# A hybrid decoder layer on one core: the third block's first product moved ahead of the first block's last one, a later fourth operand, an own tile for the last residual, more zero matmuls at the start

## The chip, the cores and the metric

The kernel runs on one core of a Trainium2 chip. The engines named below are PE (TensorE: matmuls; PEld are its weight loads), DVE (VectorE), ACT (ScalarE), POOL (GpSimd) and SP (SyncE, which issues most of the DMAs). The metric is the device time of one execution in microseconds (us), lower is better; the time before is the median of three runs.

## The reference

One layer over 1024 tokens of width 1024, in float32. `rms_norm` divides a row by its root mean square and multiplies it by a gain.

```python
def swiglu(h, w_gate, w_up, w_down):
    return (jax.nn.silu(h @ w_gate) * (h @ w_up)) @ w_down
...
        x = x + 0.5 * swiglu(rms_norm(x, ffn1_norm[i]), ffn1_w_gate[i], ffn1_w_up[i], ffn1_w_down[i])
        h = rms_norm(x, mix_norm[i])
        fq, fk, fv, f_logit, sq, sk, sv, g_fox, g_sb = split_columns(h @ w_in[i])
        ...
        merged = (jax.nn.sigmoid(g_fox) * (y_fox @ w_branch_fox[i])
                  + jax.nn.sigmoid(g_sb) * (y_sb @ w_branch_sb[i]))
        x = x + merged @ w_out[i]
        x = x + 0.5 * swiglu(rms_norm(x, ffn2_norm[i]), ffn2_w_gate[i], ffn2_w_up[i], ffn2_w_down[i])
        x = x + jax.nn.sigmoid(rms_norm(x, ple_norm[i]) @ w_ple_gate[i]) * (p[i] @ w_ple_proj[i])
```

The hidden width of the two feed-forward halves is 2816. `y_fox` and `y_sb` are two causal attentions, which the change does not touch.

## The kernel before

**Four stages of the same form.** Four large products of a normalized activation with a weight are computed by one helper, `make_up`: gate and up of the first feed-forward half (from 0 us), the gate columns of the mixer (from about 680 us), gate and up of the second half (from about 1540 us) and the gate of the last step, called PLE (from about 2160 us). What comes ahead of such a stage and fills its operands is here called its entry. In the first entry the activation comes from `x` in rows and is turned by PE; in the other three it comes from the stage before, already turned.

**Seven products a block.** The weight is cut in blocks n of 256 columns; in the feed-forward halves even n are gate columns and odd n up columns. A block's product with the activation is done as a 2 by 2 scheme with seven half-size products m = 1 to 7 in place of eight. A product is written (n, m) below. Operand B[m] of the activation is shared by all blocks; the weight's operand of (n, m) is made by `prep(n, m)`. Each operand is a float32 array split in two of a shorter format: an upper part, cast by ACT (line 649 for B, line 105 for weights), and the rest, subtracted by DVE (line 653 for B, line 106 for weights). A product is 12 matmuls of 128x512 (line 617): four with both upper parts, four with the activation's rest, four with the weight's rest.

**The order.** Nothing is scheduled by the compiler in these stages: `manual_schedule` keeps each engine in the order of the program. `up_order` lists the products; step s runs product s of that list, then `evict` of that product, then `begin(s)`, then `prep` of the product four steps later. For the blocks 1 and 2 the order is written out, with block 0 done before it without the scheme (`plain`). Step 5 is (1, 7), 6 is (2, 5), 7 is (1, 3), 8 is (2, 7) and 9 is (1, 4).

**What an eviction does.** After (n, 7) ACT copies the bank (lines 782, 1319, 1741), and DVE adds bank "d", the sum of (n, 5), to it (lines 783, 1320, 1742). The product (n, 3) goes into that same bank "d", so (1, 3) waits for this addition. In the gate blocks and in all blocks of the mixer and PLE an ACT function follows (lines 790, 1321, 1743). After (n, 1) ACT copies the bank into a new tile of `E[n]` (line 778).

**The fourth operand.** B[4] serves (n, 4) alone. It is made in four pieces j: `combo_d(j)` takes a difference in place (DVE; lines 731 and 732 in the first entry, line 734, one instruction, in the others) and `combo_e(j)` splits it (ACT 649, DVE 653). In the first entry a piece is a quarter of the tokens, so that each matmul needs all four; in the others a piece is one of the four sums over features, so that the matmuls come upon the pieces one after another. `begin(s)` calls both by the step.

**The front.** `busy(n)` issues n matmuls on a tile of zeros (line 253); the first call only clears the tile. `spread` copies the gain to all partitions by matmuls with one row (line 239), and DVE copies it back (241). Then DVE normalizes the rows (268), PE turns them (273), ACT casts (282) and DVE subtracts (287) to fill B[1] and B[2].

**The end.** In PLE the eight row blocks of the output are finished by `finish(n, i)`: a multiplication (1718), and the addition of x either inside a DMA (line 1720, issued by POOL) or on DVE (1722) with an x fetched into a tile (`fetch(..., True)`, line 1713); `store` (1726) writes it. The table `AT` says at which step each is called. `slot(tag, ...)` gives the next of a ring of buffers with that name; a new user waits for the last reader of the old one.

Of the kernel before, what the change touches and what calls it, by code (L numbers as in the profile page):

```python
# [18 lines left out]
P = 128  # L19
# [17 lines left out]
def tile_hybrid_decoder_layer(  # L37
# [484 lines left out]
                wd_sums(c, (1, 2, None, 3, 4)[i])  # L522
        return types.SimpleNamespace(sums=sums, wd_block=wd_block, wd_sums=wd_sums, load_hid=load_hid, operand=operand, prep=prep, product=product, chunks=chunks)

    def up_order(nm_):

        seqn = [(2, 1), (1, 5), (2, 2), (1, 6), (2, 6), (1, 7), (2, 5), (1, 3), (2, 7), (1, 4)]
        for n in range(3, nm_ - 1):
            seqn += [(n, 1), (n - 1, 4), (n, 2), (n - 1, 3), (n, 6), (n, 5), (n, 7)]
        n = nm_ - 1  # L530
        return seqn + [(n, 1), (n - 1, 4), (n, 2), (n, 6), (n, 5), (n, 7), (n - 1, 3), (n, 3), (n, 4)]

    def make_up(N, src, nm_, tags, first_fn, first_done=None, over=None):
# [50 lines left out]
        def last_sum(n, eng=nc.gpsimd):  # L584
            eng.tensor_sub(part(n, 2), part(n, 2), part(n, 6))
# [46 lines left out]
        def rows():  # L632
            return "rows" in N[0]
# [102 lines left out]
        def combo_e(j):  # L736
            if j == 0:
                B[4] = home(4)
            high(4, j, w(j, 0))
            low(4, j, w(j, 0))  # L740

        def begin(s):

            if s == 0:
                sums(2, nc.vector, True)
            elif s == 1:
                for q in range(4):
                    combo_s(q, 7)
            elif s == 2:
                last_sum(1, nc.vector)  # L750
            elif s == 3:
                third_sum(2, nc.vector)
            elif s == 7:
                last_sum(2, nc.vector)
            for j in range(4):
                if s == (j + 2 if rows() else 2 + j // 2):
                    combo_d(j)
            if 3 < s < 8:
                combo_e(s - 4)
        return types.SimpleNamespace(a=combo_a, b=combo_b, t=combo_t, l=combo_l, u=combo_u, s=combo_s, load=load, prep=prep, sums=sums, last_sum=last_sum, plain=plain, silu=silu, product=product, begin=begin, E=E, B=B, bank_of=bank_of)  # L760

    def ffn(N, wg, wu, wd, resid, hid, tags, entry, tail):
# [2 lines left out]
        wdown = wd[0].rearrange("(j k p) n -> k p j n", k=2, p=P)  # L765
        LA = 4
        nm_ = 2 * NF
        seqn = up_order(nm_)
        U = make_up(N, lambda n: wsrc[n % 2][:, :, n // 2 * 256:n // 2 * 256 + 256], nm_, tags, AF.Silu)
        E = U.E  # L770

        def evict(n, m, ps):
            up, j = n % 2, n // 2
            if m == 1:
                E[n] = [slot(t, [P, 2, 512]) for t in (("GF", "RN"), ("Y", "Y"))[up]]
            e1, e2 = E[n]
            if m == 1:
                nc.scalar.copy(e1[:, 0, :], ps[:])
            elif m == 6:
                nc.scalar.copy(e1[:, 1, :], ps[:])  # L780
            elif m == 7:
                nc.scalar.copy(e2[:, 1, :], ps[:])
                nc.vector.tensor_add(e2[:, 1, :], e2[:, 1, :], U.bank_of[n, "d"][:])  # L783
            elif m == 2:
                nc.vector.tensor_add(e1[:, 0, :], e1[:, 0, :], ps[:])
            elif m == 3:
                nc.vector.tensor_add(e1[:, 1, :], e1[:, 1, :], ps[:])
            if not up:
                if m == 7:
                    nc.scalar.activation(e2[:, 1, :], e2[:, 1, :], AF.Silu)  # L790
                elif m == 4:
                    nc.scalar.activation(e2[:, 0, :], ps[:], AF.Silu)
                elif m == 3:
                    nc.scalar.activation(e1[:], e1[:], AF.Silu)
                return
            g1, g2 = E[n - 1]
            if m == 7:
                nc.vector.tensor_mul(g2[:, 1, :], g2[:, 1, :], e2[:, 1, :])
            elif m == 4:
                nc.vector.tensor_mul(g2[:, 0, :], g2[:, 0, :], ps[:])  # L800
                nc.sync.dma_start(hid[j, :, 1:3, :], g2[:])
            elif m == 3:
                nc.vector.tensor_mul(g1[:], g1[:], e1[:])  # L803
                nc.sync.dma_start(hid[j, :, 0, :], g1[:, 0, :])
# [718 lines left out]
    def first_entry(F):  # L1523
# [11 lines left out]
        N.append(rows_begin(X[1], gB))  # L1535
        N[0]["B"] = [slot("H", [P, 2, 4, 512], F32R) for _ in range(2)]
        busy(0)
        busy(6)
        spread(N[0]["g"])
        for t in range(1, 4):  # L1540
            load_x(t)
# [6 lines left out]
        for t in range(4):  # L1548
            rows_stat(N[0], t, ("PT", "WL", "WL", "PT")[t], True)
            rows_mul(N[0], t)  # L1550
        busy(4)
        rows_high(N[0], 0, ps1)
        rows_high(N[0], 1, ps1)
        rows_low(N[0], 0)
# [56 lines left out]
                fn(j)  # L1611
        F.prep(1, 6)

    tags = {"raw": {1: ("KH", "KL")}, "sum": {}, "w": ("Q", "Q", "KH", "KL"), "hl": ("WL", "WL", "WL", "WH") + ("PT",) * 4 + ("WL", "WL", "WL", "PT"), "B": {"12": "X", 3: ("T",) * 4, 5: "H", 6: "H", 7: "X", 4: "X"}}
    ffn(N, ffn1_w_gate, ffn1_w_up, ffn1_w_down, xs, ad[0], tags, first_entry, mix_start())
    gqk = cp.tile([P, 1], F32, name="gqk")
    nc.sync.dma_start(gqk[0:HD, :], q_norm[0].unsqueeze(1))
# [87 lines left out]
    def ple_start():  # L1705
# [26 lines left out]
        def evict(n, m, ps):  # L1732
# [19 lines left out]
            elif m == 4:  # L1752
# [1 line left out]
        F.evict = evict  # L1754
        late = (slice(0, 512), False)
        AT = {6: [(fetch, 1, 0, "Q"), (fetch, 1, 1, "WH")], 7: [(finish, 0, 0)], 8: [(finish, 0, 1), (fetch, 3, 0, "Q", True), (fetch, 2, 1, "T")],
              9: [(fetch, 3, 0, "T")], 10: [(finish, 1, 0)], 11: [(finish, 1, 1), (fetch, 3, 1, "Q"), (store, 0, 0)], 12: [(store, 0, 1), (fetch, 3, 1, "GF", True)],
              13: [(finish, 2, 1), (fetch, 2, 0, "RAW"), (fetch, 2, 0, "RAW", True)], 14: [(finish, 3, 0, h0, *late), (store, 1, 0)], 15: [(store, 1, 1)],
              16: [(finish, 3, 1, h1, *late)], 17: [(store, 2, 1), (finish, 2, 0, slice(0, 2), *late), (finish, 3, 0, h1, *late)]}

# [58 lines left out]
```

## Time and profile before

| | |
|---|---|
| time before | 2248.29 us median of 3 runs (2247.93 to 2248.32) |
| the profiled execution | 2247.58 us, of which 2245.8 us are the span that the views show |
| PE matmul, PE weight load | 2216.0 us (99%), 1881.5 us (84%) |
| DVE, ACT, POOL | 1510.8 us (67%), 1006.0 us (45%), 820.5 us (37%) |
| mean granted TensorE clock | 0.997 of full speed |
| DMA | 298.04 MB, mean 133 GB/s |

A row of the timeline has the start in us, the duration in us, the engine, the line, the operation, the tile written and read, and how many such instructions are merged in the row; in brackets stands how long the engine sat idle before and what ended that. An engine called SPq shows the issuing of a DMA and not its transfer. Matmuls overlap, so a matmul lasts longer in the record than the distance from one to the next: 12 of them in a row take 2.88 us by the record, and the next product starts 2.72 us after.

### The profile page before, as it was taken

To read this page: it belongs to the slowest core of one execution; us is meant where nothing else is said; L and a number is where in the kernel's file an instruction comes from. 1 tells how busy PE (TensorE), PEld (TensorE's weight loads), DVE (VectorE), ACT (ScalarE), POOL (GpSimd) and SP (SyncE) were. 2 spreads that over 40 slices of the span, in tenths; PEclk is the share of its full clock that TensorE was granted. 3 is DMA by queue.
4 is the path that set the end of the run, shared out by engine and by line. 5 is a ranking of instruction groups with operands and counts; after the bars stand their busy time and mean duration, and the time that the engine had idled before them with its cause. 6 is when DMAs were issued, how large, how long until landed. Compare 5 with 4: busy or idle time off the path is not lost.

```text
span 2245.8 us, 30545 instructions
## 1 busy us (share of the span) xinstructions
PE 2216.0 (99%) x11216; PEld 1881.5 (84%) x11216; DVE 1510.8 (67%) x2366; ACT 1006.0 (45%) x1805; POOL 820.5 (37%) x787
## 2 busy tenths in 40 slices
PE   9999999999999999999999999999999999999998
PEld 7788888888888899999898888888888888888886
DVE  8754555598887324666678885889555554778897
ACT  6433333433455435555566663255333333333454
POOL 2353544210021336556566663520544354200111
PEclk9999999999999999999999999999999999999999
DMA  3332323394322334233324466741423232655327
GB/s 132 100 130 80 131 80 131 111 348 168 119 94 97 129 107 129 85 104 86 85 53 100 112 202 214 255 158 49 141 84 128 80 132 80 234 215 192 115 92 225
DMA packets 196183, 298.04 MB, mean 133 GB/s; under 512 B 28729, under 2 KB 108857, under 8 KB 196034
## 3 DMA queue, kind: packets, MB, share of 16 engines
q1 hardware_dynamic: 195312, 293.47, 39.6%
q0 software_dynamic: 720, 2.62, 0.6%
q8 instruction: 88, 1.44, 0.3%
q14 instruction: 61, 0.50, 0.1%
q10 hardware_dynamic: 2, 0.00, 0.0%
HBM read 196.14 MB, written 83.13 MB: 124 GB/s over the span
## 4 chain that ended last, share of the span: by engine, by line
PE 85%; DVE 10%; ACT 2%; issue 1%; DMA 1%; POOL 0%; DVEq 0%; ACTq 0%; POOLq 0%
PE ps L617 37%; PE ps L509 22%; PE ps L895 8%; PE ps L903 5%; PE ps L1498 4%; PE ps L1236 3%; PE ps L1210 2%; PE ps L1152 1%; PE ps L1151 1%; PE ps L561 1%; PE ps L1057 1%; DVE PT L1218 1%; DVE RN L1114 1%; DVE GF L1114 1%; DVE WL L106 1%
## 5 line engine op out<-in xcount | busy, mean ns | idle before, releaser
L509 PE MATMUL ps<-H,H 128*128 128x512 f32 x2184 | 497.3, 389 | 0.0
L509 PEld LDWEIGHTS ps<-H,H 128*128 128x128 f32 x2184 | 409.5, 188 | 84.9
L617 PE MATMUL ps<-H,WL 128*128 128x512 f32 x1176 | 278.3, 389 | 1.5 <-DVE Y L783 0.5
L617 PEld LDWEIGHTS ps<-H,WL 128*128 128x128 f32 x1176 | 220.5, 188 | 48.4 <-DVE Y L783 0.9
L185 POOL TENSOR_TENSOR PT<-PT,PT 128x512 f32<-128x512 f32 x27 | 34.9, 1294 | 403.9 <-ACT PT L182 403.0
L617 PE MATMUL ps<-H,Q 128*128 128x512 f32 x624 | 148.4, 389 | 0.0
L517 DVE SCALAR_TENSOR_TENSOR X<-ps,X 128x512 f32<-128x512 f32 x168 | 110.2, 685 | 47.4 <-PE ps L509 47.3
L617 PE MATMUL ps<-X,WL 128*128 128x512 f32 (+1 forms) x576 | 136.8, 387 | 4.4 <-ACT KH L1780 4.4
L617 PEld LDWEIGHTS ps<-H,Q 128*128 128x128 f32 x624 | 117.1, 188 | 24.3
L617 PEld LDWEIGHTS ps<-X,WL 128*128 128x128 f32 x576 | 107.6, 190 | 26.3 <-ACT KH L1780 4.6
L617 PE MATMUL ps<-H,PT 128*128 128x512 f32 x528 | 125.8, 389 | 0.0
L139 POOL TENSOR_TENSOR WL<-RAW,WH 128x512 fp32r<-128x512 f32 (+1 forms) x84 | 98.6, 1195 | 68.0 <-ACT WH L129 43.6
L1218 DVE TENSOR_TENSOR PT<-ps,PT 128x512 fp32r<-128x512 f32 (+1 forms) x160 | 100.0, 627 | 30.0 <-ACT PT L1212 29.2
L895 PE MATMUL ps<-WH,H 128*128 128x256 f32 x768 | 116.1, 287 | 0.8 <-ACT RN L960 0.8
L617 PEld LDWEIGHTS ps<-H,PT 128*128 128x128 f32 x528 | 99.0, 188 | 20.6
L903 PE MATMUL ps<-H,WH 128*128 128x512 f32 x384 | 115.0, 406 | 0.0
L1236 PE MATMUL ps<-PT,X 128*128 128x256 f32 (+1 forms) x640 | 102.3, 286 | 6.4 <-DVE PT L1218 5.5
L1212 ACT CAST PT<-ps 128x512 fp32r<-128x512 f32 (+1 forms) x160 | 87.1, 548 | 42.5 <-PE ps L1210 41.3
L1236 PEld LDWEIGHTS ps<-PT,X 128*128 128x128 f32 x640 | 90.2, 190 | 16.7 <-DVE PT L1218 10.2
L895 PEld LDWEIGHTS ps<-WH,H 128*128 128x128 f32 x768 | 101.4, 190 | 2.7 <-ACT RN L960 1.3
L412 POOL TENSOR_TENSOR PT<-GF,RN 128x512 f32<-128x512 f32 x20 | 33.7, 1686 | 190.8 <-DVE GF L803 190.8
L1164 POOL TENSOR_TENSOR T<-T,l 128x128 f32<-128x128 f32 (+3 forms) x64 | 73.3, 1148 | 71.8 <-DVE l L1163 69.8
(447 smaller groups left out, 4790.0 us busy)
## 6 DMA issues: line engine op xcount, KB each, us to landing
hidden<-PT SPq DMA_DIRECT2D x40, 512.0 KB, 2.7
WH<-in_ffn_w_gate_dram SPq DMA_DIRECT2D x38, 512.0 KB, 4.7
Q<-hidden SPq DMA_DIRECT2D x24, 512.0 KB, 6.3
hidden<-RN SPq DMA_DIRECT2D x22, 512.0 KB, 2.6
KH<-in_ffn_w_up_dram SPq DMA_DIRECT2D x20, 512.0 KB, 6.2
KL<-in_ffn_w_up_dram SPq DMA_DIRECT2D x20, 512.0 KB, 6.9
T<-in_ffn_w_down_dram SPq DMA_DIRECT2D x20, 512.0 KB, 6.2
GF<-hidden SPq DMA_DIRECT2D x14, 512.0 KB, 7.6
```

Of the source, the lines that this page charges most:

```text
L139: ins = eng_lo.tensor_sub(lo[part], raw[part], f(hi[part]))
L509: pe(nc.tensor.matmul(groups[g][t][:], wt[:, b, k, t * P:(t + 1) * P], act[:, a, k, :], start=(fresh and n == 0), stop=(i in (6, 1, 4) and ...
L517: nc.vector.scalar_tensor_tensor(xs, groups[g][t][:], scale, xs, ALU.mult, ALU.add)
L617: pe(nc.tensor.matmul(ps[:, cols], hl[:, a, k, :], right(B[m], b, k)[:, cols], start=(first and i == 0), stop=(final and i == 11), skip_gr ...
L895: pe(nc.tensor.matmul(ps[:, :n], hT[t // 4](a, k)[:, (t % 4) * P:(t % 4 + 1) * P], w[k // 4][b][:, k % 4, :n], start=(i == 0), stop=(i == ...
L903: pe(nc.tensor.matmul(ps[:], w[a][:, k, :], hT[half](b, k), start=(i == 0), stop=(i == 23)))
L1114: order("dve", nc.vector.tensor_tensor_scan(*args))
L1164: nc.gpsimd.tensor_mul(T[:, :n], T[:, :n], l[:].broadcast_to([P, n]))
L1212: high = nc.scalar.copy(pt[:, 0, :width], ps[:, :width])
L1218: ins = nc.vector.tensor_sub(pt[:, 1, :width], ps[:, :width], f(pt[:, 0, :width]))
L1236: pe(nc.tensor.matmul(o, lh, r, start=(kpair == c and i == 0), stop=(kpair == 0 and i == 3)))
L1498: pe(nc.tensor.matmul(ps[:], w[a][:, k, :], yT[g][b][:, k, half * 512:half * 512 + 512], start=(i == 0), stop=(i == 11)))
```

## The change

- In the first entry (`rows`), (3, 1) is put ahead of (1, 4): step 9 is now (3, 1) and step 10 is (1, 4). `E[3]` gets two buffers of the ring `T`, since those of `Y` still hold block 1's.
- In the first entry `combo_d(j)` moves from steps 2, 3, 4, 5 to 3, 4, 5, 6 and `combo_e(j)` from 4, 5, 6, 7 to 6, 7, 8, 9; the third call for block 2, `last_sum(2)`, moves from step 7 to 8.
- In the other three entries `combo_d(2)` and `combo_d(3)` move from step 3 to 5, and `combo_e(j)` from 4, 5, 6, 7 to 5, 6, 7, 8.
- In PLE the x of the last output rows goes into a tile of `KL` at step 9, no longer into one of `GF` at step 12.
- `busy(6)` becomes `busy(8)` ahead of `spread`, and `busy(4)` becomes `busy(10)` ahead of the first turning.
- The list that names the buffers of the weight operands in the first feed-forward half is six entries longer, with `WH` at place 15 (that of (3, 1)).

```diff
-    def up_order(nm_):
+    def up_order(nm_, rows=False):
 
         seqn = [(2, 1), (1, 5), (2, 2), (1, 6), (2, 6), (1, 7), (2, 5), (1, 3), (2, 7), (1, 4)]
+        if rows:
+            seqn.insert(-1, (3, 1))
         for n in range(3, nm_ - 1):
-            seqn += [(n, 1), (n - 1, 4), (n, 2), (n - 1, 3), (n, 6), (n, 5), (n, 7)]
+            seqn += [(n, 1)][rows and n == 3:] + [(n - 1, 4), (n, 2), (n - 1, 3), (n, 6), (n, 5), (n, 7)]
...
-            elif s == 7:
+            elif s == (8 if rows() else 7):
                 last_sum(2, nc.vector)
+            d_at, e_at = ((3, 4, 5, 6), (6, 7, 8, 9)) if rows() else ((2, 2, 5, 5), (5, 6, 7, 8))
             for j in range(4):
-                if s == (j + 2 if rows() else 2 + j // 2):
+                if s == d_at[j]:
                     combo_d(j)
-            if 3 < s < 8:
-                combo_e(s - 4)
+            for j in range(4):
+                if s == e_at[j]:
+                    combo_e(j)
...
-                E[n] = [slot(t, [P, 2, 512]) for t in (("GF", "RN"), ("Y", "Y"))[up]]
+                E[n] = [slot(t, [P, 2, 512]) for t in tags.get("E", {}).get(n, (("GF", "RN"), ("Y", "Y"))[up])]
...
-        busy(6)
+        busy(8)
         spread(N[0]["g"])
...
-        busy(4)
+        busy(10)
...
-              9: [(fetch, 3, 0, "T")], 10: [(finish, 1, 0)], 11: [(finish, 1, 1), (fetch, 3, 1, "Q"), (store, 0, 0)], 12: [(store, 0, 1), (fetch, 3, 1, "GF", True)],
+              9: [(fetch, 3, 0, "T"), (fetch, 3, 1, "KL", True)], 10: [(finish, 1, 0)], 11: [(finish, 1, 1), (fetch, 3, 1, "Q"), (store, 0, 0)], 12: [(store, 0, 1)],
```

Three places show how instructions move. The changed file has two more lines ahead of `begin` and four more behind it, so line 649 of before is 651 there, 653 is 655, 783 is 787 and 1321 is 1325.

First, DVE in the first entry, from line 783's addition (the one that (1, 3) waits for) to the piece j = 3 of B[4], the row that reads KL. Before:

```order
L783 TENSOR_TENSOR Y_443<-Y_443,ps_573 128x512
L798 TENSOR_TENSOR RN_341<-RN_341,Y_443 128x512
L731 TENSOR_TENSOR KL_399<-H_107,KL_399 128x512
L732 TENSOR_TENSOR KL_399<-KL_399,H_107 128x512
L653 TENSOR_TENSOR X_656<-Q_321,X_656 128x4x128
L106 TENSOR_TENSOR Q_681<-KL_137,Q_681 128x512
L653 TENSOR_TENSOR X_656<-KH_364,X_656 128x4x128
L106 TENSOR_TENSOR Q_699<-KH_637,Q_699 128x512
L787 TENSOR_TENSOR Y_442<-Y_442,ps_573 128x512
L803 TENSOR_TENSOR GF_340<-GF_340,Y_442 128x1024
L585 TENSOR_TENSOR WH_348<-WH_348,RAW_567 128x4x128
L653 TENSOR_TENSOR X_656<-KL_399,X_656 128x4x128
```

Now the last eleven rows up to that piece are these. Between the addition and them stand nine more, by their new lines 802, a pair 733 and 734, 106, a second such pair, 655, 106 and 791:

```order
L807 TENSOR_TENSOR GF_348<-GF_348,Y_450 128x1024
L655 TENSOR_TENSOR X_700<-Q_329,X_700 128x4x128
L106 TENSOR_TENSOR PT_723<-WH_356,PT_723 128x512
L787 TENSOR_TENSOR RN_573<-RN_573,ps_685 128x512
L587 TENSOR_TENSOR WH_356<-WH_356,RAW_575 128x4x128
L655 TENSOR_TENSOR X_700<-KH_372,X_700 128x4x128
L578 TENSOR_TENSOR RAW_744<-KH_643,KL_644 128x512
L579 TENSOR_TENSOR RAW_744<-RAW_744,KH_643 128x512
L584 TENSOR_TENSOR KH_643<-KH_643 128x4x128
L106 TENSOR_TENSOR WL_748<-KL_644,WL_748 128x512
L655 TENSOR_TENSOR X_700<-KL_407,X_700 128x4x128
```

Between the addition and the last piece stood 10 instructions on DVE; now there stand 19. Of the work ahead of the addition, one pair 731 and 732 and one 653 have gone behind it; the sums of block 3 (lines 576, 577 and 582 of before) now stand ahead of the last piece.

Second, ACT in the mixer's entry (the other two have the same order there), from the copy and the function of (1, 7) to those of (2, 7), both on a tile RN. Before:

```order
L1321 ACTIVATE RN_4972<-RN_4972 128x512
L649 CAST X_5190<-Q_4935 128x512
L105 CAST Q_5213<-WH_4672 128x512
L649 CAST X_5190<-KH_4941 128x512
L105 CAST Q_5231<-WH_5173 128x512
L1326 ACTIVATE GF_4971<-GF_4971 128x1024
L649 CAST X_5190<-KH_4947 128x512
L105 CAST PT_5252<-RAW_4839 128x512
L1319 COPY RN_5098<-ps_5084 128x512
L1321 ACTIVATE RN_5098<-RN_5098 128x512
```

Now the end of that stretch reads:

```order
L1330 ACTIVATE GF_4979<-GF_4979 128x1024
L651 CAST X_5216<-KH_4949 128x512
L105 CAST PT_5258<-RAW_4847 128x512
L1323 COPY RN_5106<-ps_5092 128x512
L1325 ACTIVATE RN_5106<-RN_5106 128x512
L651 CAST X_5216<-KH_4955 128x512
```

The cast of the last piece (KH_4947 before, KH_4955 now) stood ahead of the copy of (2, 7) and now stands behind the function of (2, 7).

Third, SP at the end of PLE, where DMAs wait in a queue. Before:

```order
L1726 DMA out_dram<-GF_18858 128x1024
L1726 DMA out_dram<-RN_18859 128x1024
L1713 DMA GF_19330<-x_end 128x1024
L1713 DMA RAW_19350<-p_proj 128x1024
L1713 DMA RAW_19352<-x_end 128x1024
L1726 DMA out_dram<-KH_19282 128x512
```

The fetch of x has left its place behind the two stores:

```order
L1717 DMA T_19275<-p_proj 128x1024
L1717 DMA KL_19277<-x_end 128x1024
L1717 DMA Q_19318<-p_proj 128x1024
L1730 DMA out_dram<-GF_18866 128x1024
L1730 DMA out_dram<-RN_18867 128x1024
```

It now goes into KL and is issued ahead of the first store.

More of the change, by code (lines that the diff above doesn't have):

```diff
@@ L767, in ffn @@
         nm_ = 2 * NF
-        seqn = up_order(nm_)
+        seqn = up_order(nm_, "w" in tags)
         U = make_up(N, lambda n: wsrc[n % 2][:, :, n // 2 * 256:n // 2 * 256 + 256], nm_, tags, AF.Silu)
@@ L1612, in first_entry @@
         F.prep(1, 6)
-    tags = {"raw": {1: ("KH", "KL")}, "sum": {}, "w": ("Q", "Q", "KH", "KL"), "hl": ("WL", "WL", "WL", "WH") + ("PT",) * 4 + ("WL", "WL", "WL", "PT"), "B": {"12": "X", 3: ("T",) * 4, 5: "H", 6: "H", 7: "X", 4: "X"}}
+    tags = {"raw": {1: ("KH", "KL")}, "sum": {}, "w": ("Q", "Q", "KH", "KL"), "E": {3: ("T", "T")}, "hl": ("WL", "WL", "WL", "WH") + ("PT",) * 4 + ("WL", "WL", "WL", "PT", "WL", "WL", "WL", "WH", "Q", "PT"), "B": {"12": "X", 3: ("T",) * 4, 5: "H", 6: "H", 7: "X", 4: "X"}}
     ffn(N, ffn1_w_gate, ffn1_w_up, ffn1_w_down, xs, ad[0], tags, first_entry, mix_start())
```

## The prediction

> **What bounds the kernel now.** I read the page's busy shares first, then the list of what PE waited for, then the timeline around each long wait, and last the granted clock there.
>
> ```profile
> PE 2216.0 (99%) x11216; PEld 1881.5 (84%) x11216; DVE 1510.8 (67%) x2366; ACT 1006.0 (45%) x1805; POOL 820.5 (37%) x787
> ...
> PE ps L617 <- ACT KH L1780: 4.4, 1, 4.4
> PE ps L617 <- DVE Y L783: 3.0, 2, 2.5
> ...
> PE ps L617 <- DVE RN L1742: 0.5, 1, 0.5
> PE ps L617 <- DVE RN L1320: 0.5, 1, 0.5
> ```
>
> The first line gives busy time, share and instructions; the others who waited for whom, total us, times, longest us. PE never rests for long, so a change is worth what it adds to or takes from PE's few holes, and from what stands before the first product and after the last one. The change aims at five holes: before (1, 3) 2.5 us at the first entry and 0.5 us in each of the others (line 783's 3.0 us are two of them), and 4.4 us at the end.
>
> The first hole costs more than its 2.5 us. The rows are PE's in the first entry: (1, 3), (2, 7) and (1, 4).
>
> ```profile
> 69.21 4.61 PE L617 MATMUL ps<-T,WL 128*128 128x512 f32 x12 [2.48 <-DVE Y L783]
> 73.65 2.89 PE L617 MATMUL ps<-X,WL 128*128 128x512 f32 x12
> 76.38 2.88 PE L617 MATMUL ps<-X,Q 128*128 128x512 f32 x12
> ```
>
> From (2, 7) to (1, 4) are 2.73 us, the normal distance; (1, 3) took 4.61 us where 2.89 is normal. The granted clock explains that (stretch, its length, PE, PEld, DVE, ACT, POOL, then PEclk, DMA share, GB/s):
>
> ```profile
> 70.50:71.00 0.50, 0.50 (x2) 0.41 (x2) 0.49 (x1) 0.00 (x0) 0.00 (x0) 0.50 0.00 0
> 73.00:73.50 0.50, 0.50 (x3) 0.41 (x2) 0.50 (x2) 0.50 (x1) 0.00 (x0) 0.50 0.03 10
> ```
>
> After the hole PE ran at half clock for about three us. So a hole of 2.48 us cost 2.48 + 1.72 = 4.2 us, and any new hole of that length may be followed by such a loss too.
>
> **The first entry, products (1, 3) to (3, 1).** DVE is what ends last there:
>
> ```profile
> 61.47 0.69 DVE L731 TENSOR_TENSOR Q<-H,Q 128x512 f32<-128x512 f32 x1
> 62.80 0.69 DVE L106 TENSOR_TENSOR WL<-RAW,WL 128x512 fp32r<-128x512 f32 x1
> 67.27 0.68 DVE L653 TENSOR_TENSOR X<-Q,X 128x512 fp32r<-128x512 f32 x1
> 68.47 0.68 DVE L783 TENSOR_TENSOR Y<-Y,ps 128x512 f32<-128x512 f32 x1
> 74.57 1.23 DVE L803 TENSOR_TENSOR GF<-GF,Y 128x1024 f32<-128x1024 f32 x1
> 76.32 0.68 DVE L653 TENSOR_TENSOR X<-KL,X 128x512 fp32r<-128x512 f32 x1
> ```
>
> A pair 731 and 732 takes 62.80 - 61.47 = 1.33 us, and two plain instructions 68.47 - 67.27 = 1.20, so 0.60 each. Ahead of the addition at line 783 one pair and one 653 are taken away, 1.9 us, so it ends at 67.25 instead of 69.15. That is the gain: PE's hole before (1, 3) shrinks from 2.5 to about 0.6 us.
>
> The loss is behind it. (1, 4) now comes one product later, but its operand's last piece comes much later: 20 instructions after the addition where 11 were. They are three pairs (two 731 and 732, and 576 with 577) at 1.33, the dependent 787 and 803 at 0.7 + 1.2, and twelve plain ones at 0.60: 4.0 + 1.9 + 7.2 = 13.1 us, against 77.00 - 69.15 = 7.85 us before. So the rest of the last piece is ready at 67.25 + 13.1 = 80.4 instead of 77.0. Eight of (1, 4)'s twelve matmuls need it (1.8 us at 2.72 us for 12), and so (1, 4) ends at 82.2. Before, (1, 4) and then (3, 1) started at 76.38 and were done by 76.38 + 2 x 2.72 = 81.8. Both orders have done the same products at that point: **+0.4 us**, with no half clock counted. What the moved product gives PE is used up: three products from 67.3 end at 75.4, and there (1, 4) stands. The cast of its last piece waits on ACT behind the copy of (3, 1) and the function of (2, 7). That function's addition stands on DVE behind two pairs, the double addition and seven plain instructions, itself the last: 2.7 + 1.9 + 4.2 = 8.8 us after 67.25, at 76.0. The function, three instructions of ACT and the cast, 0.5 to 0.6 us each, then end at about 78.9: a hole of 3.5 us, and one of 0.6 behind the fourth matmul, where the rest is waited for. Bounds: if DVE gets 2 us ahead somewhere, -1.5; with DVE or ACT waiting for each other, +1.
>
> **The three other entries.** The mixer's entry is the plain one:
>
> ```profile
> 702.10 2.88 PE L617 MATMUL ps<-X,WL 128*128 128x512 f32 x12
> 708.30 1.07 PE L617 MATMUL ps<-T,WL 128*128 128x512 f32 x4
> ...
> 710.70 0.60 ACT L649 CAST X<-KH 128x512 fp32r<-128x512 f32 x1
> 711.02 2.88 PE L617 MATMUL ps<-X,Q 128*128 128x512 f32 x12
> 711.73 0.58 ACT L1319 COPY RN<-ps 128x512 f32<-128x512 f32 x1
> 712.54 0.69 DVE L1320 TENSOR_TENSOR RN<-RN,ps 128x512 f32<-128x512 f32 x1
> 713.26 0.64 ACT L1321 ACTIVATE RN<-RN 128x512 f32<-128x512 f32 x1 [0.96 <-DVE RN L1320]
> 713.80 0.61 ACT L105 CAST WL<-WH 128x512 fp32r<-128x512 f32 x1
> ```
>
> (2, 5) starts at 702.10 and (2, 7) at 708.30, two products and a hole later: the hole costs 6.20 - 2 x 2.72 = 0.76 us. Moving two differences (line 734) and one 653 behind the addition takes 1.9 us off DVE ahead of it, so this hole goes.
>
> What is late next is the last piece. Before, its cast at 710.70 stood ahead of (2, 7)'s copy. Now it stands behind (2, 7)'s function: copy, addition on DVE, function, cast. From the rows, the instruction behind the function starts 713.80 - 711.73 = 2.07 us after the copy, and the cast takes 0.6: 2.7 us, to which some 0.2 from (1, 4)'s possible start to (2, 7)'s copy are added (2.88 recorded less 2.72, and a releasing of 0.04 as in the row of line 241 below). (1, 4) follows (2, 7) at once, its first three matmuls (0.7 us) need the other pieces, and the fourth waits: 2.9 - 0.7 = 2.2 us. Net 2.2 - 0.76 = **+1.4 us**. In the second feed-forward half DVE also has the double addition's long product ahead of (2, 7)'s addition, and in PLE a finishing multiplication:
>
> ```profile
> 1570.25 1.22 DVE L803 TENSOR_TENSOR GF<-GF,Y 128x1024 f32<-128x1024 f32 x1
> 2208.22 1.22 DVE L1718 TENSOR_TENSOR GF<-GF,T 128x1024 f32<-128x1024 f32 x1
> ```
>
> Going through DVE's new order with 0.60 an instruction, the addition waits about 0.5 us for the first and 1.2 for the second: holes of 2.7 and 3.4 us, net **+1.9** and +2.6 us. PE is the bound right before and after, so the first two pass to the end. Bounds for each: -0.8, if the cast came in time after all, to the hole alone, +2.7 and +3.4.
>
> **The end.** PE, DVE and the queue of SP:
>
> ```profile
> SPq L1713 <- DMA out_dram<-GF: 6.3, 1, 6.3
> ...
> 2231.18 1.59 PE L617 MATMUL ps<-X,WL 128*128 128x256 f32 x12
> 2234.89 0.69 DVE L1722 TENSOR_TENSOR KH<-KH,GF 128x512 f32<-128x512 f32 x1 [4.94 <-DMA GF<-x_end]
> 2235.50 0.68 DVE L1749 TENSOR_TENSOR KH<-KH,ps 128x512 f32<-128x512 f32 x1
> 2237.17 2.58 PE L617 MATMUL ps<-X,WL 128*128 128x256 f32 x12 [4.40 <-ACT KH L1780]
> 2241.17 0.42 DVE L1722 TENSOR_TENSOR KH<-KH,GF 128x256 f32<-128x256 f32 x1
> ```
>
> The fetch into GF waited 6.3 us in SP's queue for a store out of GF, DVE stood 4.94 us for it, and PE behind DVE and ACT. With its own tile the fetch goes at step 9, and DVE's 1749 needs only (3, 3), which is done 0.2 us after 2231.18, at about 2231.4: 4.1 us earlier than 2235.50. What follows it on DVE is 2241.59 - 2235.50 = 6.1 us long and stays. But PLE's PE is 2.6 us late by then, which leaves -1.5. And the DMA engines are full:
>
> ```profile
> 2224.00:2226.00 2.00, 2.00 (x11) 1.65 (x10) 1.41 (x3) 0.06 (x1) 0.89 (x1) 1.00 1.05 252
> 2240.00:2242.00 2.00, 0.00 (x0) 0.00 (x0) 1.52 (x5) 0.17 (x1) 0.00 (x0) 0.50 1.03 416
> ```
>
> Their share is 1.05 and 1.03, and the same bytes still have to go. By that the end would not move at all. Between -1.5 and 0 I take **-0.9 us** for PLE and the end together; the bounds are -4.1, if PLE's hole does not come, and +1.
>
> **The front.** PE's zeros, spread and turning, and the DVE copy that waits for the spread:
>
> ```profile
> 1.32 2.74 PE L253 MATMUL ps<-T 128*128 128x512 bf16 x6 [1.32 <-DVE T L249]
> 4.06 3.75 PE L239 MATMUL ps<-PT,T 1*128 1x512 f32 x4
> 7.74 1.89 PE L253 MATMUL ps<-T 128*128 128x512 bf16 x4
> ...
> 7.85 0.69 DVE L241 COPY PT<-ps 128x512 f32<-128x512 f32 x1 [1.01 <-PE ps L239]
> 9.98 1.97 PE L273 MATMUL ps<-identf,PT 128*128 128x128 f32 x8 [0.35 <-DVE PT L268]
> 11.74 2.11 PE L273 MATMUL ps<-identf,WL 128*128 128x128 f32 x16
> ```
>
> Six zeros fill 2.74 us, 0.43 a step by the first and last. Two more push spread and everything on DVE by 0.85 us. Ten instead of four behind it end at 7.74 + 0.85 + 10 x 0.43 = 12.9, where the turning could start at 9.98: 2.9 us late. The turnings got twice as fast at about 11.74 (8 in 1.97, then 16 in 2.11), so starting later they run fast at once, 0.9 us less for the first eight. Between +0.85 and +2.0 I take **+1.5 us**, nearer to the turnings' row, since the casts follow them; it passes on, because DVE, which ends last at 69 us, works from there on nearly without a gap.
>
> Below that is one case. In these rows PE was busy from 1.32 to 9.63 without a gap and slow all the time; it became fast only after zeros and turnings of full size. Eight zeros in a row are 8 x 0.43 = 3.4 us of such work. If they release the clock ahead of spread, its 3.75 us halve: -1.9 + 0.85 = -1.0, of which DVE's waits for the third row block leave perhaps -0.6. That is a rival below.
>
> [...]
>
> **The clock after new holes.** The one hole of 2.48 us was followed by a loss of 1.72 us, those of 0.8 us by none. New holes are 3.5, 2.2, 2.7 and 3.4 us. I count one loss, **+1.7 us**, for the first entry, whose hole is longer than the one measured. Bounds 0 and 3 x 1.7 (PLE's lies in front of a full DMA queue).
>
> **Edits that I cost at nothing.** WH at place 15 makes block 4's second load wait for block 2's last weight operand; (4, 1) comes six products, 16 us, behind (1, 4), which covers it. If not, PE waits for a DMA there, some 2 us. E[3] in T: its two buffers were last read by the zeros and the spread, in the first 13 us.
>
> **Sum.** 0.4 + 1.4 + 1.9 - 0.9 + 1.5 + 1.7 = +6.0 us. The profiled execution took 2247.58 us, so 2253.6; the median of the runs is 0.7 above it, so 2254.3 on its scale. A measurement of this kernel can tell about 0.2%, 4.5 us, from no change: faster is below 2243.8, slower above 2252.8.
>
> **Rivals.**
> - *The fourth operand is in time, and the holes just go.* It decides when the last piece's cast is done before the fourth matmul of (1, 4), 2.2 us earlier than I work out. For it: the view names DVE or ACT as what ended each of the holes aimed at. Against: ACT runs in program order, and the rows show the copy, addition and function one after another. Price: -4.2, -0.8, -0.8, the end -3 between its bounds, the front 0: -8.8, so 2238.8 + 0.7 = 2239.5. Chance 0.08.
> - *The front runs fast.* The eight zeros release the clock before the spread. For it: 16 turnings at half the price show a release about 2 us after full-size work resumed. Against: six zeros did not do it. -0.6 in place of +1.5: 3.9, so 2252.2. Chance 0.23.
> - *Each new hole is followed by half clock.* For it: both holes above 2 us in this trace were (the last 12 matmuls of 256 columns took 2.58 us against 1.59). Against: the holes here are shorter in two entries. Two more losses of 1.7: +9.4, so 2257.7. Chance 0.2.
> - *No new hole in the first entry*, since DVE gets ahead: -1.5 there in place of 0.4, and no loss of clock: 6.0 - 1.9 - 1.7 = 2.4, so 2250.7. Chance 0.12.
>
> My forecast has the remaining 0.37. Faster by over 0.2% is the first rival: 0.08. Within 0.2% are the fourth and most of the second, 0.12 + 0.15, and the lower edge of the forecast, 0.05: 0.32. Slower: 0.60. The range, 2247.0 to 2259.5, leaves out the first rival (0.08) and the outermost part of the third (about 0.1), where PLE's loss comes on top; it takes in the bounds of the first entry and of the end one at a time.
>
> **What would show it.** Right: in the list of PE's waits, line 783 below 1 us, and new waits at 617 for ACT's line 651 of 2 us or more in each of the three entries, and one for DVE's 655 or ACT in the first; no wait at the end for line 1780 over 1 us; the granted clock at 0.50 behind the first of them. The chain of waits shows the copy, addition, function and cast in a row. Wrong: (1, 4) follows (2, 7) without a hole in the mixer's entry, or spread's matmuls at half their 0.94 us each, or the end earlier by over 3 us.

## The result, and the profile after

The changed kernel takes 2265.95 us (median of 4 runs, 2265.42 to 2267.61) against 2248.31 beside it: ratio 1.008, 95% interval 1.0062 to 1.0097. It is slower by 17.6 us where the prediction had 6.0, and above its range. The profiled execution took 2265.42 us with a span of 2263.7, 17.9 more than that of before.

The list of what PE waited for in the changed kernel (total us, times, longest us):

```profile
PE ps L619 <- ACT X L651: 15.6, 5, 4.7
PE ps L619 <- DVE X L655: 0.6, 1, 0.6
PE ps L619 <- DVE Y L787: 0.6, 1, 0.6
PE ps L619 <- ACT KH L1784: 0.5, 1, 0.5
```

The four holes that the change aimed at outside the end are gone or, at the first entry, down to 0.6 us; the end's fell from 4.4 to 0.5. In their place stand five waits for line 651, the cast of the fourth operand, 15.6 us together. The timeline of PE shows them: spread; then the first entry from (2, 5) to (3, 2), the mixer from (2, 5) to (2, 4), the second feed-forward half and PLE, each from (1, 7) to (2, 4).

```profile
4.57 1.98 PE L239 MATMUL ps<-PT,T 1*128 1x512 f32 x4
...
63.11 2.88 PE L619 MATMUL ps<-H,WL 128*128 128x512 f32 x12
...
72.19 2.88 PE L619 MATMUL ps<-H,WH 128*128 128x512 f32 x12
78.90 1.72 PE L619 MATMUL ps<-X,Q 128*128 128x512 f32 x4 [3.82 <-ACT X L651]
81.24 3.78 PE L619 MATMUL ps<-X,Q 128*128 128x512 f32 x8 [0.62 <-DVE X L655]
...
88.20 2.88 PE L619 MATMUL ps<-H,WL 128*128 128x512 f32 x12
...
705.76 2.88 PE L619 MATMUL ps<-X,WL 128*128 128x512 f32 x12
...
713.92 0.61 PE L619 MATMUL ps<-X,Q 128*128 128x512 f32 x2
715.51 0.50 PE L619 MATMUL ps<-X,Q 128*128 128x512 f32 x1 [0.97 <-ACT X L651]
718.60 4.21 PE L619 MATMUL ps<-X,Q 128*128 128x512 f32 x9 [2.59 <-ACT X L651]
...
726.21 2.88 PE L619 MATMUL ps<-X,PT 128*128 128x512 f32 x12
...
1571.59 2.88 PE L619 MATMUL ps<-T,PT 128*128 128x512 f32 x12
...
1582.47 0.84 PE L619 MATMUL ps<-X,Q 128*128 128x512 f32 x3
1588.05 3.89 PE L619 MATMUL ps<-X,Q 128*128 128x512 f32 x9 [4.74 <-ACT X L651]
...
1594.54 2.88 PE L619 MATMUL ps<-X,PT 128*128 128x512 f32 x12
...
2212.10 2.88 PE L619 MATMUL ps<-H,PT 128*128 128x512 f32 x12
...
2222.98 0.84 PE L619 MATMUL ps<-X,PT 128*128 128x512 f32 x3
2227.25 4.21 PE L619 MATMUL ps<-X,PT 128*128 128x512 f32 x9 [3.43 <-ACT X L651]
...
2234.90 2.89 PE L619 MATMUL ps<-X,PT 128*128 128x512 f32 x12
```

The same products in the timeline of before, where the prediction did not show them:

```profile
63.84 2.88 PE L617 MATMUL ps<-H,WL 128*128 128x512 f32 x12
...
84.54 2.88 PE L617 MATMUL ps<-H,WL 128*128 128x512 f32 x12
...
716.47 2.88 PE L617 MATMUL ps<-X,PT 128*128 128x512 f32 x12
...
1560.36 2.88 PE L617 MATMUL ps<-T,PT 128*128 128x512 f32 x12
...
1577.48 2.88 PE L617 MATMUL ps<-X,PT 128*128 128x512 f32 x12
...
2195.04 2.88 PE L617 MATMUL ps<-H,PT 128*128 128x512 f32 x12
...
2212.14 2.88 PE L617 MATMUL ps<-X,PT 128*128 128x512 f32 x12
```

The differences of these starts split the 17.9 us. The last two columns give the recorded waits for the fourth operand, and what is left of the new time from (1, 4) on (in the first entry from (3, 1) on) after the matmuls, 0.227 us each as before, and these waits: the slow clock, and about 0.2 us for each restart, an estimate from the second half (1.9 us left, of which half clock for 3.41 us, shown below, makes 1.7).

| stretch | before | after | difference | forecast | new waits | left |
|---|---|---|---|---|---|---|
| start to (2, 5), the front | 63.84 | 63.11 | -0.73 | +1.5 | | |
| first entry, (2, 5) to (3, 2) | 20.70 | 25.09 | +4.39 | 0.4 + 1.7 | 4.44 | 3.4 |
| mixer, (2, 5) to (2, 4) | 14.37 | 20.45 | +6.08 | +1.4 | 3.56 | 3.3 |
| mixer to second half | 843.89 | 845.38 | +1.49 | 0 | | |
| second half, (1, 7) to (2, 4) | 17.12 | 22.95 | +5.83 | +1.9 | 4.74 | 1.9 |
| PLE, (1, 7) to (2, 4) | 17.10 | 22.80 | +5.70 | -0.9 | 3.43 | 3.1 |
| (2, 4) to the end | 33.66 | 28.80 | -4.86 | (with PLE) | | |

For the last column, in the mixer: 726.21 - 713.92 = 12.29 us for 24 matmuls of 5.44 and 3.56 of waits. The 1.49 us between mixer and second half are not of the change: no line of it runs there, and the same stretch takes anything from 843.6 to 845.5 us in the profiles of this document's runs. The granted clock, in short stretches of the mixer and of the second half (stretch, length, PE, PEld, DVE, ACT, POOL, PEclk, DMA share, GB/s):

```profile
717.70:717.80 0.10, 0.00 (x0) 0.00 (x0) 0.00 (x0) 0.10 (x1) 0.00 (x0) 0.50 0.00 0
724.30:724.40 0.10, 0.10 (x2) 0.08 (x1) 0.10 (x1) 0.00 (x0) 0.00 (x0) 0.50 1.23 492
1587.90:1588.00 0.10, 0.00 (x0) 0.00 (x0) 0.00 (x0) 0.10 (x2) 0.00 (x0) 1.00 0.00 0
1591.50:1591.60 0.10, 0.10 (x2) 0.06 (x2) 0.00 (x0) 0.00 (x0) 0.10 (x1) 1.00 0.00 0
```

In the mixer the clock was at half for 6.83 us, 717.62 to 724.44, and the wait ended only at 718.60, inside it. In the second half it was at half for 3.41 us, 1588.02 to 1591.43, and the wait ended at 1588.05, as it began. The sum had one of the holes followed by half clock. All four were, and three of them for twice as long as the old hole (70.16 to 73.58): the first entry from 79.32 to 86.15 and PLE from 2226.31 to 2233.13, like the mixer.

### The profile page after: what moved, and what is told of

Read it like the earlier page. It is cut to its first block, busy times and chain, and to the rows that moved or that the text cites. A ratio compares the mean times of both kernels' runs of the same rounds, so it can differ in the third digit from the quotient of the medians.

```text
span 2263.7 us, 30562 instructions
## 1 busy us (share of the span) xinstructions
PE 2223.6 (98%) x11224; PEld 1885.4 (83%) x11224; DVE 1507.6 (67%) x2366; ACT 1006.2 (44%) x1805; POOL 821.2 (36%) x787
## 5 line engine op out<-in xcount | busy, mean ns | idle before, releaser
L619 PE MATMUL ps<-X,Q 128*128 128x512 f32 x372 | 96.3, 408 | 12.8 <-ACT X L651 12.1
```

What stands on the lines that cost most here:

```text
L619: pe(nc.tensor.matmul(ps[:, cols], hl[:, a, k, :], right(B[m], b, k)[:, cols], start=(first and i == 0), stop=(final and i == 11), skip_gr ...
```

## The experiments

The kernel before, measured beside each of these, had medians of 2247.5 to 2248.0; beside the changed kernel's 2265.95 it had 2248.31. Counted by the kernel before, which was that much faster beside these runs, a gain over 2265.95 is 0.4 to 0.8 us smaller than the plain difference.

| run | us (lowest to highest) | ratio to before (95%) |
|---|---|---|
| e1, three later entries back | 2253.32 (2250.3 to 2254.48) | 1.0023 (1.0014 to 1.0032) |
| e2, first entry back | 2260.01 (2258.86 to 2261.59) | 1.0056 (1.0043 to 1.0068) |
| e3, x alone | 2247.54 (2246.96 to 2249.16) | 1.0000 (0.9991 to 1.0009) |
| e4, zeros alone | 2248.91 (2247.34 to 2251.14) | 1.0007 (0.9998 to 1.0016) |
| e5, middle steps | 2246.55 (2246.18 to 2248.13) | 0.9995 (0.9986 to 1.0004) |
| e6, first entry, splits earlier | 2244.80 (2244.39 to 2245.25) | 0.9986 (0.9977 to 0.9995) |
| e7, holes filled | 2260.49 (2257.86 to 2261.56) | 1.0053 (1.0039 to 1.0067) |
| e8, PLE back | 2265.15 (2263.23 to 2266.51) | 1.0075 (1.0063 to 1.0088) |
| e10, weights in PT | 2260.74 (2258.88 to 2262.88) | 1.0057 (1.0043 to 1.0070) |
| f1, old hole filled | 2248.30 (2247.16 to 2248.81) | 1.0000 (0.9991 to 1.0009) |
| c1, e5 and e6 | 2244.24 (2243.41 to 2245.67) | 0.9982 (0.9973 to 0.9991) |
| c2, c1 and x at step 8 | 2242.69 (2241.22 to 2242.94) | 0.9974 (0.9963 to 0.9985) |

**e1, the three later entries back.**

```diff
-            d_at, e_at = ... if rows() else ((2, 2, 5, 5), (5, 6, 7, 8))
+            d_at, e_at = ... if rows() else ((2, 2, 3, 3), (4, 5, 6, 7))
```

> The changed kernel with the fourth operand of the mixer, the second feed-forward half and PLE back at its old steps (differences at 2, 2, 3, 3, splits at 4, 5, 6, 7). Theory (the late fourth operand opens a hole in each of the three entries, and each hole is followed by half clock): the three entries give back 6.08 + 5.83 + 5.70 = 17.6 us, so 2265.95 - 17.6 = 2248.3. Rival (at the end the DMA engines bound the time once PLE is no longer late, so that PLE's 5.7 us don't come back): 2254.

2253.3: 12.6 us come back (11.9 by the kernel before), not 17.6, so my first account of the end was wrong and the rival right. The late operand in mixer and second half (11.9 in the table) explains nearly all of it; PLE's 5.7 did not return.

**e8, PLE alone back**, by the same edit, put on PLE only.

> The changed kernel with the old steps of the fourth operand in PLE alone (2, 2, 3, 3 and 4, 5, 6, 7). Theory (the DMA engines bound the end, so PLE's 5.7 us were hidden but for 5.7 - 4.9 = 0.8): 2265.1. Rival (the end follows PE, as the sum of the prediction had it): 2265.95 - 5.7 = 2260.3.

2265.15, 0.8 below the changed kernel as worked out; that little is not told from nothing, but the rival's 2260.3 is ruled out. PLE's hole lies in front of work that waits for the DMA engines anyway: their share is 1.02 to 1.06 from 2242 to 2262 us in the changed kernel.

**e3, x alone**, on the kernel before.

```diff
-              9: [(fetch, 3, 0, "T")], ...
+              9: [(fetch, 3, 0, "T"), (fetch, 3, 1, "KL", True)], ...
-              12: [(store, 0, 1), (fetch, 3, 1, "GF", True)],
+              12: [(store, 0, 1)],
```

> The kernel before with one edit: the last x goes into a tile of KL at step 9, no longer into one of GF at step 12. Theory (the end was waiting for that fetch alone): the hole of 4.4 us shrinks to about 0.5 and the half clock there goes, 4.9 us, so 2243.4. Rival (with PLE not late, the full DMA engines bound the end): 2247 to 2249.

The time is that of before. PE's hole of 4.4 us is 0.5 in this run, and yet the end stands: DVE, in the timeline of this run, now waits as long for another landing.

```profile
2236.16 1.23 DVE L1718 TENSOR_TENSOR Y<-Y,RAW 128x1024 f32<-128x1024 f32 x1 [4.50 <-DMA RAW<-p_proj]
```

The -4.86 us of the table are therefore not a gain of the fetch into KL. From the start of (1, 7) in PLE to the end it is 2245.8 - 2195.04 = 50.8 us before and 2263.7 - 2212.10 = 51.6 in the changed kernel: PE came 5.7 us later in between, and the end, which waits for the DMA engines (share 1.02 to 1.06 from 2218 to 2242 us in this run), hardly did.

**e2, the first entry back**, the zeros kept.

```diff
-        seqn = up_order(nm_, "w" in tags)
+        seqn = up_order(nm_)
-            elif s == (8 if rows() else 7):
+            elif s == 7:
-            d_at, e_at = ((3, 4, 5, 6), (6, 7, 8, 9)) if rows() else ...
+            d_at, e_at = ((2, 3, 4, 5), (4, 5, 6, 7)) if rows() else ...
```

The lists of buffers (`E`, `hl`) go back too.

> The changed kernel with the first entry as before: (3, 1) behind (1, 4), differences, splits and the third sum at their old steps, E[3] in Y, the old list of weight buffers; the zeros stay. Theory (the moved product and the later operand cost 4.4 us there, the zeros gain 0.7): 2265.95 - 4.4 = 2261.6, with the hole of about 2.5 us before (1, 3) back. [...]

2260.0: the first entry's part of the change costs 5.9 us, of which the two profiles, both with a fast front, show 4.3 between (2, 5) and (3, 2). The profiles differ by 6.4 us in all. Of the rest 1.1 lie in the mixer and 1.8 in the stretch between mixer and second half, which varies by that much from run to run. Neither belongs to the first entry.

**e4, the zeros alone**, on the kernel before (`busy(8)`, `busy(10)`).

> The kernel before with one edit: 8 and 10 zeros in place of 6 and 4. Theory (eight zeros release the clock ahead of the spread, whose matmuls then take half the time): -0.7 us, so 2247.6, and the hole before (1, 3) stays. Rival, the price of my sum (they only push the front back): +1.5, so 2249.8.

+1.4, close to the price of my sum, but the interval reaches just below 1. What decides is in the timelines: the row of spread in e4, and in e3, which has the old front.

```profile
4.85 3.78 PE L239 MATMUL ps<-PT,T 1*128 1x512 f32 x4
```

```profile
4.23 2.14 PE L239 MATMUL ps<-PT,T 1*128 1x512 f32 x4 [0.16 <-DMA PT<-in_ffn_norm_dram]
```

With the new front, spread took 3.78 us in e4 and 1.98 in the profile of the changed kernel; with the old one 3.75 in that of before and 2.14 in e3. The same front finds a slow or a fast PE at 4 us from one execution to the next, with six zeros as with eight. By the start of (2, 5), a fast spread with the new front is worth -0.73 against before, and a slow one costs +1.7 (65.56 in e4 against 63.84). So the forecast's term and its rival are both true, by run, but the fast spread is not owed to the eight zeros: with six and a fast spread (2, 5) starts at 63.47 (e3). Why one execution has a fast spread and another a slow one, no run here shows.

**e7, the new holes filled**, on the changed kernel.

```diff
+            fill = tags["fill"].get((n, m))
+            if fill:
+                fps = bank("av")
...
+                    if fill and i in fill:
+                        for _ in range(fill[i]):
+                            pe(nc.tensor.matmul(fps[:], hl[:, 0, 0, :], right(B[m], 0, 0), start=True, stop=True))
...
```

> The changed kernel with matmuls into an unused bank placed into the new holes, as many as fill them (17 behind (3, 1) and 4 inside (1, 4) in the first entry; 5 and 12 inside (1, 4) in the mixer, 21 in the second half, 15 in PLE). Nothing reads them. Theory (the half clock behind the holes is the larger part of the miss: 3.0, 2.8, 1.6 and in PLE 2.8, of which the end passes on 0.8 at most): 2265.95 - 3.0 - 2.8 - 1.6 - 0.8 = 2257.7, and the granted clock stays at 1.00 in all four entries. Rival (the half clock comes from something else than the idle PE): it stays, and the time is 2266 or more.

74 matmuls whose result nobody reads make the kernel 5.5 us faster (2260.49 against 2265.95; 4.9 by the kernel before). The clock, in the stretches of this run over the mixer's and PLE's holes:

```profile
715.00:724.00 9.00, 9.00 (x41) 7.04 (x40) 6.69 (x9) 4.48 (x9) 1.29 (x1) 1.00 0.34 118
...
2220.00:2230.00 10.00, 9.97 (x44) 7.93 (x43) 8.49 (x11) 3.88 (x7) 4.09 (x3) 1.00 0.67 162
```

It stays at 1.00. The run profiled has a slow front, 2.1 us behind the changed kernel's at (2, 5); the three earlier entries took 2.3, 2.7 and 1.6 us less from (3, 1) or (1, 4) on, about what was worked out. PLE's took 2.7 less, and the end took 2.2 of it back, with a wait of 1.43 us of DVE for RAW.

**e10, the weights cast between the splits in other buffers**, on the changed kernel. ACT's rows in the changed kernel, the copy of (2, 7) in the mixer first, then the second half and PLE:

```profile
715.88 0.58 ACT L1323 COPY RN<-ps 128x512 f32<-128x512 f32 x1
...
1577.86 0.62 ACT L651 CAST X<-Q 128x512 fp32r<-128x512 f32 x1 [2.77 <-DVE KH L736]
1579.24 0.62 ACT L105 CAST Q<-WH 128x512 fp32r<-128x512 f32 x1 [0.76 <-DVE X L655]
...
1581.22 0.62 ACT L105 CAST Q<-WH 128x512 fp32r<-128x512 f32 x1 [0.84 <-DVE X L655]
...
2217.61 0.62 ACT L651 CAST X<-Q 128x512 fp32r<-128x512 f32 x1 [0.57 <-DVE KH L736]
2218.14 0.62 ACT L105 CAST PT<-WH 128x512 fp32r<-128x512 f32 x1
```

In the second half the weight's cast (line 105) goes into a buffer of Q and waits until DVE's line 655 has read the piece that was there; in PLE it goes into PT and does not wait.

```diff
+        hl[15:17] = ["PT", "PT"]
...
-"hl": ("WL", "WL", "WL", "KL") + ("PT",) * 4 + ("WL", "WL", "WL", "PT"), "B": HOMES}
+"hl": ("WL", "WL", "WL", "KL") + ("PT",) * 4 + ("WL", "WL", "WL", "PT", "WL", "WL", "WL", "PT", "PT", "PT"), "B": HOMES}
```

> The changed kernel with the two weight operands that ACT casts between the splits of the fourth operand (Q in the mixer and in the second half) put into buffers of PT, as PLE has them. Theory (in the ring of Q such a buffer is the tile that the split before it has just read, so ACT waits for DVE and DVE for ACT, 0.7 us each time; PLE, where they are in PT, had the hole of 3.4 us that I had worked out, the other two had more): the holes come to the worked-out 2.2 us in the mixer (4.0 measured between the matmuls) and 2.7 in the second half (4.9), with one window of half clock or two behind each as before: 2265.95 - 1.8 - 2.2 = 2262. Rival (the holes are set by the eviction's chain alone): 2266, with the same holes.

5.2 us faster than the changed kernel (4.8 by the kernel before), a little more than expected. PE's holes in this run, mixer and second half, and then the clock in short stretches behind each.

```profile
717.28 3.63 PE L619 MATMUL ps<-X,PT 128*128 128x512 f32 x9 [2.27 <-ACT X L651]
...
1583.14 2.34 PE L619 MATMUL ps<-X,PT 128*128 128x512 f32 x9 [3.19 <-ACT X L651]
```

```profile
718.05:718.10 0.05, 0.05 (x1) 0.00 (x1) 0.05 (x1) 0.00 (x0) 0.00 (x0) 0.50 0.00 0
721.30:721.38 0.08, 0.08 (x2) 0.08 (x1) 0.00 (x0) 0.08 (x1) 0.08 (x1) 0.50 0.00 0
721.42:721.50 0.08, 0.08 (x2) 0.04 (x2) 0.00 (x0) 0.08 (x2) 0.08 (x1) 1.00 0.00 0
...
1583.20:1583.70 0.50, 0.50 (x2) 0.42 (x3) 0.50 (x1) 0.50 (x2) 0.00 (x0) 1.00 0.00 0
1585.00:1585.50 0.50, 0.50 (x4) 0.42 (x3) 0.50 (x2) 0.00 (x0) 0.00 (x0) 1.00 0.00 0
```

The mixer's 3.56 us became 2.27, what I had worked out; the second half's 4.74 became 3.19, still 0.5 above the 2.7. And the hole of 3.19 us was followed by no half clock at all (1.00 at 1583.2 and at 1585.0), its nine matmuls taking 2.34 us, while the mixer's of 2.27 was (0.50 from 718.05 to 721.38), with 3.63 for the same nine. So the length of a hole alone does not tell whether half clock follows; what does, no run here shows. The 5.2 us are then not all owed to the buffers: in the profiles the two holes are 2.8 us shorter, and the two entries lose 3.0 us less to the clock, one stretch of 3.41 us (a window, in the expectation) less in each. That second part may be luck, since a shorter hole was hit and a longer one was not.

**f1, the old hole filled**, on the kernel before: 11 such matmuls behind (2, 5) of the first entry.

> The kernel before with 11 matmuls into an unused bank behind (2, 5) of the first entry, in the hole of 2.48 us before (1, 3); nothing reads them. Theory (the half clock behind that hole costs 1.7 us and comes from PE standing still): 2247.7 - 1.7 = 2246.0 and the granted clock stays at 1.00. Rival (the 11 matmuls only take the place of the hole, or delay (1, 3)): 2247.7 or more.

The clock stayed at 1.00, as the stretch shows, and nothing was gained: PE met a new wait in (1, 4).

```profile
70.00:70.50 0.50, 0.50 (x4) 0.40 (x3) 0.50 (x2) 0.00 (x0) 0.00 (x0) 1.00 0.00 0
```

```profile
76.96 2.11 PE L617 MATMUL ps<-X,Q 128*128 128x512 f32 x8 [0.88 <-DVE X L657]
```

In that stretch DVE's last split ended last, with the hole or without. The half clock of before was mostly hidden behind it: from (2, 5) to (3, 2) this run took 20.29 us, the kernel before 20.70.

**e6, the first entry with earlier splits**, on the kernel before: the moved product, its buffers and the step of `last_sum(2)` as in the change, and

```diff
-            d_at, e_at = ((3, 4, 5, 6), (6, 7, 8, 9)) if rows() else ...
+            d_at, e_at = ((3, 4, 5, 5), (5, 5, 6, 7)) if rows() else ...
```

> The kernel before with one edit in the first entry: (3, 1) ahead of (1, 4) with its buffers as in the change, but differences at 3, 4, 5, 5 and splits at 5, 5, 6, 7 in place of 3 to 6 and 6 to 9. Theory (the moved product was right, the splits were late): the hole before (1, 3) shrinks to about 0.6, 13 instructions of DVE behind the addition, about 8.8 us, end by 76.5 when (1, 4) starts at 75.4 to 76.3, and the half clock goes; (2, 4) starts at about 78.2 in place of 81.82: 2247.5 - 3.6 = 2243.9. Rival (DVE bounds the entry whatever the order): a hole of 2 us or more before (1, 4) with half clock, 2247 to 2249.

2244.80, 3.0 us faster than before. (1, 4) and (2, 4) in its timeline:

```profile
75.55 2.88 PE L619 MATMUL ps<-X,Q 128*128 128x512 f32 x12
78.27 2.88 PE L619 MATMUL ps<-X,PT 128*128 128x512 f32 x12
```

(1, 4) has no wait, and (2, 4) starts at 78.27 in place of 81.82, as worked out.

**e5 and c1, splits at 5, 5, 6, 7 in the later entries**, on the kernel before and on e6.

> The kernel before with one edit in the three later entries: differences at steps 2, 2, 5, 5 as in the change, but splits at 5, 5, 6, 7, so that the last split stands where it stood before. Theory (the holes came from the last split standing behind the eviction of (2, 7), not from the later differences): the holes of 0.7 us before (1, 3) go and none opens before the fourth matmul; PLE's share is lost at the full DMA engines, so 2247.5 - 1.4 = 2246.1. Rival (the shared buffers of Q make ACT and DVE wait for each other, and the last split is late all the same): holes over 1 us with half clock behind them, 2250 or more.

> The kernel before with the two edits that paid by themselves: the first entry of e6 (the moved product, splits at 5, 5, 6, 7) and the later entries of e5 (differences at 2, 2, 5, 5, splits at 5, 5, 6, 7). Theory (different stages, so they add): 2247.7 - 3.0 - 1.2 = 2243.5. Rival (one of them only shifts the end into the full DMA engines): 2244.8, as e6 alone.

By itself e5 is not told from nothing (interval 0.9986 to 1.0004), and c1 is only 0.6 us below e6. The profile of e5 gives the mixer 0.5 us less, and the second half 0.2 more, since (1, 4) waits 0.7 us for the rest of the last piece there. The 1.4 expected was too much.

**c2, x fetched at step 8 into KL**, on c1.

```diff
-              8: [(finish, 0, 1), (fetch, 3, 0, "Q", True), ...
+              8: [(finish, 0, 1), (fetch, 3, 1, "KL", True), (fetch, 3, 0, "Q", True), ...
-              12: [(store, 0, 1), (fetch, 3, 1, "GF", True)],
+              12: [(store, 0, 1)],
```

> c1 with the last x in a tile of KL as in the change, but fetched at step 8 ahead of the fetches that wait for a buffer, where the DMA engines have idle time (16 and 0 GB/s around 2208 us), and not at step 9 among the full ones. Theory (the bytes that must go through the full engines set the end): 0.5 MB less there at about 270 GB/s, 1.9 us, so 2241.6 to 2242. Rival (the end is set by the last landings whatever is taken away ahead of them): as c1, 2243.5.

2242.69, 1.6 below c1 and the fastest of all (0.9974, 0.9963 to 0.9985, to before). The same stretch of PLE in c1 and in c2:

```profile
2204.00:2208.00 4.00, 4.00 (x19) 3.29 (x19) 3.96 (x6) 1.91 (x5) 1.07 (x1) 1.00 0.48 154
```

```profile
2204.00:2208.00 4.00, 4.00 (x19) 3.31 (x18) 3.96 (x7) 2.44 (x5) 1.06 (x1) 1.00 0.92 292
```

The DMA share there rises from 0.48 to 0.92, before the stretch of full engines (0.98 to 1.04 from 2208 to 2220 us in c2); a part of that is c2's PLE starting 1.4 us earlier in its profile, and from 2200 to 2212 us the mean share is 0.78 in c1 and 0.87 in c2. The direction is as expected: the slowest time of c2, 2242.94, is below the fastest of c1, 2243.41. The intervals of the two overlap, so the size isn't settled; in the two profiles PLE, from (1, 7) on, takes 50.3 and 49.3 us. Step and tile changed together here, and c1 with KL at step 9 was not run; on the kernel before that tile alone gained nothing (e3).

## Why the prediction was wrong

- **The clock after new holes** is the step that failed most: "I count one loss, +1.7 us, for the first entry." Each of the four holes was followed by half clock, 3.4, 3.3, 1.9 and 3.1 us by the table. Two errors are in it. The rival that was right in this got 0.2 for its chance, against a row that spoke for it, and counted no loss in PLE; and a loss was sized by the one hole of before, which ended at 69.21 us, before the half clock began at 70.16. Where the wait reached into the half clock, by 0.98 us in the mixer and 0.94 in PLE, or a second wait fell there, 0.62 us in the first entry, it lasted 6.83 us; in the second half, with 0.03 us of the wait in it, 3.41. With the holes filled the clock stayed at 1.00 (e7), so the cause is PE standing still. That all four holes were hit may be luck in part: one of 3.19 us in e10 was not.
- **The hole sizes** came out in PLE (3.43 us for 3.4) and nearly in the first entry (3.82 and 0.62 for 3.5 and 0.6). In the mixer (3.56 for 2.2) the failing step was "some 0.2 from (1, 4)'s possible start to (2, 7)'s copy": (1, 4) starts at 713.92 and the copy at 715.88, 1.96 us later, and from there to the end of the cast are the 2.7 us of the forecast. In the second half (4.74 for 2.7) it was "Going through DVE's new order with 0.60 an instruction", which let DVE run without a pause. Behind both stands the weight's buffer in Q, which made ACT and DVE take turns (ACT's waits of 0.76 and 0.84 us in the second half); e10 takes 1.3 and 1.55 of the misses of 1.4 and 2.0 away. The first entry's +0.4 came out at 1.0 without the clock (4.39 - 3.4): there DVE waits for ACT twice as well, 0.69 and 0.60 us, which the sum had only as a bound.
- **The order of events was right**: the holes before (1, 3) went, the last piece's cast came behind copy, addition and function of (2, 7), and the first entry lost at (1, 4).
- **The end**: "By that the end would not move at all" was the right reading, and -0.9 for PLE and the end together the wrong sum of it; +0.8 was measured (5.70 - 4.86), inside its bounds. In the kernel before, the fetch in SP's queue was what PE waited for, but not what bounded the end (e3).
- **The front**: +1.5 and the rival's -0.6 both occur, as e4 and the changed kernel's profile show. The error was to treat it as one answer, and the rival's, to lay the fast spread to eight zeros.
- **"So a hole of 2.48 us cost 2.48 + 1.72"** does not hold as a price: f1 took the half clock away and gained nothing. What e6 saved came with work of DVE moved behind the addition and one more product ahead of (1, 4); no run takes these two apart.
- The edits costed at nothing show no wait of their own: (3, 1) starts at 72.19, one distance of 2.72 behind (2, 7), and from (3, 2) to the mixer's (2, 5), which has (4, 1) in it, both kernels take 617.56 us.

## What to carry to other kernels

Before an operand is made later, write down what stands on ACT and DVE between its steps and whose buffers these write to; in a ring shared with the operand's pieces ACT waited 0.76 and 0.84 us for DVE here, in the second half, and with the weights in PT (e10) the hole there was 3.19 us in place of 4.74. Count a hole in a full PE at its length, and allow for half clock behind it: here it came behind holes of 2.27 us (e10) to 4.74 us (the changed kernel), lasted 3.41 or 6.83 us and took 1.72 us before and 1.9 to 3.4 by the table, and behind one of 3.19 us (e10) it did not come. And before a wait at the end is removed, look at the DMA share there: at 1.0 the wait was worth nothing here (e3), and what shortened the end moved bytes to before that stretch (c2).

## What was not expected of the hardware

- Stretches of half clock between full ones were 3.41 us (1588.02 to 1591.43) or 6.83 us long (717.62 to 724.44) in the changed kernel. In the three longer ones PE stood for 0.62 to 0.98 us after the clock had fallen, in the shorter one for 0.03.
- Whether a hole is followed by half clock, and for how long, is not told by its length: the second half's hole of 4.7 us cost one stretch in the changed kernel, the mixer's of 2.27 one and the second half's of 3.19 none in e10.
- PE was fast or slow at 4 us from execution to execution of the same front (spread 1.98 us in the changed kernel, 3.78 in e4). With the new front (2, 5) starts at 63.1 to 63.5 us when it is fast (63.11 in the changed kernel, 63.52 in e2) and at 65.2 to 65.8 when it is slow (65.56 in e4, 65.79 in e8).
